# Where the tiles begin: one residue modulo 256 bytes for all of SBUF, another for the weights of the 256-column products

## The chip, the cores and the metric

The kernel runs on one core of a Trainium2 chip. The metric is device time in microseconds of one execution: before the change the median of three runs is 1165.34 us (1165.07 to 1167.91). One further execution was profiled; the rows shown below are from it.

## What is computed

A two-layer decoder trunk on 512 tokens of width 1024, in float32. Layer 0 mixes with a gated DeltaNet (six heads), layer 1 with a sliding-window attention (12 query heads, 2 key/value heads), both add an attention into 256 memory tokens, and both end in a feed-forward block of width 2816. The two feed-forward blocks hold most of the matrix work:

```python
def swiglu(h, w_gate_up, w_down):
    gu = h @ w_gate_up
    return (jax.nn.silu(gu[..., :D_FF]) * gu[..., D_FF:]) @ w_down

for layer in range(DEPTH):
    h = rms_norm(x, ln_mix[layer])
    ...
    x = x + jnp.concatenate([mix_out, mem_o], axis=-1) @ w_out[layer]
    x = x + swiglu(rms_norm(x, ln_ffn[layer]), w_gate_up[layer], w_down[layer])
    ...
return rms_norm(x, ln_final)
```

## The kernel before

Activations are kept transposed, features on the 128 partitions and the 512 tokens along the free dimension. Every float32 matrix product is made of three products of rounded operands: an operand is split into a high part (ScalarE, `copy` at L138) and the rest (VectorE, L151), and `mm3` adds high by high, high by low and low by high into one PSUM bank. In these products the weight part is the stationary operand (a 128 by 128 piece of a tile `whi` or `wlo`), and the activation part (`h`, `l`, `ac8h`, `T` and so on) streams through TensorE as the moving operand. Nearly all of TensorE's time is in two sizes of such products:

- **512 columns.** `project` (input projections, output projections, the first four gate tiles of a feed-forward block) and the down products of `ffn`, all into banks named `pj` (some `g` and `sc`). The weights come through `weight`, which takes a pair of tiles of 1024 columns from the pool `w`, three buffers each.
- **256 columns.** All other gate and up products of `ffn` go through `quarters`, which computes two column tiles of the weights by two halves of the tokens with seven products in place of eight. Each product is four `mm3`, twelve matmuls of 256 columns into a bank `g`. Its moving operands are halves of `h` or the sums of `token_sums` (tiles `T`). Its weights are split by `ring` into halves of the same `whi`/`wlo` tiles: a tile of 1024 columns holds two places of 512.

Two stretches of `quarters` lie in each feed-forward block, each followed by down products; at the end of layer 1 the last two down tiles are computed in token halves, so in 256 columns too.

**Where a tile lies.** Pools open on the left side of SBUF (`const`, `w`, `acta`, `actb`, `x`) grow upwards from the constants; pools opened on the right (`layer0`, `early`, `gdn`, `ffn0`, `swa`, `ffn1`) grow downwards from the top. A tile's length is rounded up to 32 bytes by the allocator, and nearly all large tiles are a multiple of 256 bytes long, so the few short ones decide the residue of all that follow. In the built program the tiles of `w`, `acta`, `actb` and `x` begin at 96 modulo 256, those on the right mostly at 224. A weight piece begins a multiple of 512 bytes into its tile, and a moving operand at its tile's beginning or 1024 bytes into it, so the residue of an operand is that of its tile:

| matmuls in high and low parts | moving operand | weights | count |
|---|---|---|---|
| 512 columns | 96 | 96 | 2112 |
| 512 columns (`ac8` to `ac11`, and the memory output of layer 0) | 224 | 96 | 324 |
| 256 columns (most of them on `T`) | 224 | 96 | 2028 |
| 256 columns (most of them on `h`) | 96 | 96 | 1488 |
| 256 columns (last down tile) | 96 | 224 | 144 |
| 256 columns (the rest) | 224 | 224 | 12 |

**The sum of squares.** For each RMS norm, `accumulate` squares a tile on ScalarE and adds it on VectorE to a running sum; each sum goes to the other of two buffers `sqa`. `rstd_from` sums it over the partitions with one matmul by ones.

**Smaller tiles.** `token_sums` keeps a column of negated gains (`minus`) and a half tile `fc`; `scores` and `weigh` keep `mx`, `den`, `nm`, `es`; `solve` keeps `Y32` and `Y64`, three buffers each. The order on each engine comes from the scheduler of the tile layer, which follows the program where nothing waits.

Of the kernel before, what the change touches and what calls it, by code (L numbers as in the profile page):

```python
# [18 lines left out]
P = 128  # L19
# [7 lines left out]
DFF = 2816  # L27
FT = DFF // P
EPS = 1e-6
NEG = -1e30  # L30
BASE = 32
NB = P // BASE
# [54 lines left out]
class Builder:  # L87
# [6 lines left out]
    def t(self, pool, shape, dtype=F32, tag=None, bufs=None, name=None):  # L94
        self.n += 1
        nm = f"{name or tag}_{self.n}"
        kw = {}
        if tag is not None:
            kw["tag"] = tag
        if bufs is not None:  # L100
            kw["bufs"] = bufs
        return pool.tile(shape, dtype, name=nm, **kw)

    @contextmanager
# [69 lines left out]
    def load(self, src, pool=None, bufs=2):  # L174
# [2 lines left out]
        self.nc.sync.dma_start(raw, src)  # L177
        return raw

    def weight(self, src, eng=None, raw=None, parts=1, pool=None, tags=("whi", "wlo"), bufs=3):  # L180

        raw = self.load(src) if raw is None else raw
        n = raw.shape[1]
        hi = self.t(pool or self.wpool, [P, D], F32R, tags[0], bufs)[:, :n]
        lo = self.t(pool or self.wpool, [P, D], F32R, tags[1], bufs)[:, :n]
        for i in range(parts):
            s = slice(i * n // parts, (i + 1) * n // parts)
            self.split(raw[:, s], hi[:, s], lo[:, s], eng or self.weng)
        return hi, lo
# [37 lines left out]
    def build(self):  # L227
        tc, nc, a = self.tc, self.nc, self.a
        with ExitStack() as st:
            opened = lambda name, **kw: tc.tile_pool(name=name, bufs=1, reuse_waits="tile", **kw)  # L230
            pool = lambda name, **kw: st.enter_context(opened(name, **kw))
            cp = pool("const")
            self.wpool, self.apool = pool("w"), pool("acta")
            self.dpool = pool("scratch", space=DRAM)
            self.load_constants(cp)
            self.weng = nc.vector
            with opened("layer0", side="right") as self.mpool:
                with self.banks(pj=3, g=2, sc=3):
                    with opened("early", side="right") as ep:
                        self.mem_and_norm(ep)  # L240
                        self.gates(ep)
                    with opened("gdn", side="right") as gp:
                        mix = self.gdn(gp)
                    self.bpool, xp = pool("actb"), pool("x")
                    self.x = [self.t(xp, [P, T], F32, f"x{k}") for k in range(KD)]
                    for k in range(KD):
                        nc.sync.dma_start(self.x[k], a["xT"][:, k, :])
                    self.rstd, self.cosT, self.sinT = (self.t(xp, [P, T], F32, n) for n in ("rstd", "cosT", "sinT"))
                    h = self.output(xp, 0, mix, self.bpool)
            with opened("ffn0", side="right") as fp, self.banks(pj=2, g=6):  # L250
                self.ffn(fp, xp, 0, h, self.apool, rope=True)
            with self.banks(pj=2, g=1, qk=1, pt=2, sc=1):
                with opened("swa", side="right") as sp:
                    mix = self.swa(sp)
                h = self.output(xp, 1, mix, self.apool)
            with opened("ffn1", side="right") as fp, self.banks(pj=2, g=6):
                self.ffn(fp, xp, 1, h, self.bpool)

    def load_constants(self, cp):
        nc, a = self.nc, self.a  # L260
        c = self.t(cp, [P, C_N], F32, "consts")
        g = self.t(cp, [P, G_N], F32, "gains")
        s = self.t(cp, [P, 24], F32, "small")
        nc.sync.dma_start(g, a["gains"])
        self.consts, self.gains, self.small = c, g, s
        self.ident = c[:, C_ID:C_ID + P]
        self.U = c[:, C_U:C_U + P]
        self.ones = c[:, C_ONE:C_ONE + P]
        self.caus = c[:, C_CAUS:C_CAUS + P]
        self.band = c[:, C_BAND:C_BAND + 2 * P]  # L270
        self.one = c[:, C_ONE:C_ONE + 1]
        v = self.t(cp, [P, 2], F32, "eps")
        nc.vector.memset(v[:, 0:1], EPS)
        nc.vector.memset(v[:, 1:2], EPS * EPS * P)
        self.eps, self.epsq = v[:, 0:1], v[:, 1:2]
# [376 lines left out]
    def solve(self, gp, heads, Ns, X64, Tts):  # L652

        nc = self.nc
        Xs = [X64[:, h * NC:(h + 1) * NC, :] for h in heads]
        part = lambda ps, a, w: ps[:, a * w * NC:(a + 1) * w * NC].rearrange("p (c m) -> p c m", c=NC)
        for B, starts in ((BASE, (0, 2 * BASE)), (2 * BASE, (0,))):
            pairs = [(slice(s, s + B), slice(s + B, s + 2 * B)) for s in starts]
            banks = [self.bank("sc") for _ in heads]
            ys = [self.t(gp, [P, NC, B], F32, f"Y{B}", 3) for _ in heads]  # L660
            for ps, N, X, y in zip(banks, Ns, Xs, ys):
                for a, b in pairs:
                    for c in range(NC):
                        self.mm(part(ps, 0, B)[b, c, :], N[a, c, b], X[a, c, 0:B])
                for a, b in pairs:
                    nc.vector.tensor_copy(y[b], part(ps, 0, B)[b])
            for ps, X, y, Tt in zip(banks, Xs, ys, Tts):
                for a, b in pairs:
                    for c in range(NC):
                        if B == BASE and a.start == 0:  # L670
                            self.mm(part(ps, 1, B)[b, c, :], Tt[b, c, b], y[b, c, :])
                        self.mm(part(ps, 2 if B == BASE else 1, B)[a, c, :], y[b, c, :], Tt[b, c, b])
                for a, b in pairs:
                    if B == BASE and a.start == 0:
                        self.ts(X[b, :, 0:B], part(ps, 1, B)[b], -1.0, ALU.mult)
                    self.ts(Tt[a, :, b], part(ps, 2 if B == BASE else 1, B)[a], -1.0, ALU.mult)
# [33 lines left out]
    def scores(self, pool, q, kk, win):  # L710
# [3 lines left out]
        half = [slice(0, 64), slice(64, P)]  # L714
        sm = [self.t(pool, [P, 2, 2, 2 * P], F32, "sm", 4 if own else 2) for _ in range(2)]
        sm = [t[:, n] for t in sm for n in range(2)]
        mx = self.t(pool, [P, 2 * NC], F32, "mx", 2)
        den = self.t(pool, [P, 2 * NC], F32, "den", 2)
        nm = self.t(pool, [P, 2 * NC], F32, "nm", 2)
        for n0 in range(0, NC, 2):  # L720
            if own:
                two = self.bank("qk", [P, 2, 2, 2 * P])
# [8 lines left out]
            for b in range(2):  # L731
# [14 lines left out]
        return sm, mx, den, nm  # L746

    def weigh(self, pool, scores, vv, m, out, sinks):

# [1 line left out]
        win = sinks is not None  # L751
        own = "pt" in self.pbufs
        half = [slice(0, 64), slice(64, P)]
        sm, mx, den, nm = scores
        if win:
            sk = sinks.unsqueeze(2).to_broadcast([P, 2, NC])
            v4 = lambda ap: ap.rearrange("p (b n) -> p b n", b=2)
            self.stt(v4(mx), v4(mx), 0.125, sk, ALU.mult, ALU.max)
            self.ts(nm, mx, -1.0, ALU.mult)
            es = self.t(pool, [P, 2 * NC], F32, "es", 2)  # L760
# [49 lines left out]
    def output(self, xp, layer, mix, hpool):  # L810
# [5 lines left out]
        for m in range(KD):  # L816
# [6 lines left out]
            self.acc = self.accumulate(xp, self.acc, self.x[m], m)  # L823
        return h

    def ffn(self, fp, xp, layer, h, apool, rope=False):
# [22 lines left out]
        def ring():  # L849

            if not places:
                for _ in range(3):
                    two = [self.t(self.wpool, [P, D], F32R, t, 3) for t in ("whi", "wlo")]
                    places.extend(tuple(x[:, i * T:(i + 1) * T] for x in two) for i in range(2))
            places.append(places.pop(0))
            return places[-1]

# [22 lines left out]
        for f0, half in ((0, 12), (12, 10)):  # L880
# [16 lines left out]
            for m in range(tail):  # L897
# [5 lines left out]
                        self.mm3(ps, w, k, acts[j + k], j + k == 0, j + k == half - 1)  # L903
                add(self.x[m], ps)
                if f0:
                    self.acc = self.accumulate(xp, self.acc, self.x[m], m)
                if rope and f0 == 0 and m == 0:
                    self.rope_tables(fp)
        if tail < KD:
# [9 lines left out]
            for t in parts:  # L919
                acc = self.acc[:, t]  # L920
                for m in range(tail, KD):
# [5 lines left out]
                    sq = self.t(fp, [P, T], F32, "fg", 4)[:, t]  # L927
                    self.square(sq, x)
                    if m < KD - 1:
                        nxt = self.t(xp, [P, T], F32, "sqa", 2)[:, t]  # L930
                        self.tt(nc.vector, nxt, acc, sq, ALU.add)
                        acc = nxt
                ends.append(self.final(fp, (acc, sq), t))
            for (ps, r), o, t in zip(ends, outs, parts):
                self.store(ps, r, o, t, tail)
# [1 line left out]
    def token_sums(self, fp, layer, j, h):  # L937
# [77 lines left out]
        self.mm(ps, self.ones, acc)  # L1015
        self.rsqrt(self.rstd[:, t], ps, D)

    def accumulate(self, pool, acc, x, m, out=None):

        n = x.shape[1]  # L1020
        sq = self.t(pool, [P, T], F32, "sq", 2)[:, :n]
        self.square(sq, x)
        if acc is None:
            return sq
        nxt = self.t(pool, [P, T], F32, "sqa", 2) if out is None else out
        self.tt(self.nc.vector, nxt, acc, sq, ALU.add)
        return nxt

    def rope_tables(self, pool):

# [192 lines left out]
```

## Time and profile before

| | us |
|---|---|
| median of the runs | 1165.34 |
| the profiled execution | 1165.44 |
| its span, first to last instruction | 1163.7 |
| TensorE (PE) busy | 1139.6 (98%) |
| weight loads (PEld) busy | 997.3 (86%) |
| VectorE (DVE) busy | 843.7 (73%) |
| ScalarE (ACT) busy | 635.8 (55%) |
| share of PE in the chain that ended last | 88% |

Matmuls are pipelined and their ends are modelled in the profile: a product of 256 columns is shown with a duration near 280 ns although the next one starts about 120 ns later. What a product costs is therefore read from how many of them follow each other in a piece of the chain, not from the mean duration of its group. The granted TensorE clock was 0.997 of full over the whole execution.

### The profile page before, as it was taken

Reading aid. Unit: us, or ns where it says so; the run is one execution under the profiler, and the core shown is the slowest. Engines: PE = TensorE matmul, PEld = TensorE weight load, DVE = VectorE, ACT = ScalarE, POOL = GpSimd, SP = SyncE. Lnnn points to the kernel's source line nnn. Section 1 sums busy time; section 2 is a strip of 40 time slices with the busy share of each in tenths; the row PEclk is TensorE's granted clock in tenths of the full one; section 3 lists DMA queues with packets and bytes.
Section 4 is the critical chain, followed back from the end, with each engine's and each line's share of the span. In section 5 each row is a group of like instructions: output and inputs, shape, how many; then the busy total and the mean of one; then the engine's idle time right before and its main releaser. Section 6 shows DMA issues by size and latency. Waiting matters only on the chain.

```text
span 1163.7 us, 19670 instructions
## 1 busy us (share of the span) xinstructions
PE 1139.6 (98%) x7476; PEld 997.3 (86%) x7476; DVE 843.7 (73%) x1587; ACT 635.8 (55%) x1273; POOL 85.9 (7%) x97
## 2 busy tenths in 40 slices
PE   7999999999999999999999999999999999999996
PEld 6888777877899998899998777678999988999986
DVE  5754877767789887378866767859799843898754
ACT  7569563366556652256654547675566522566533
POOL 0310000000101100011100000010011100111000
PEclk9999999999999999999999999999999999999998
DMA  8434352224657744567723421143477733577232
GB/s 307 135 101 115 113 127 92 74 90 163 170 142 187 183 127 124 148 148 179 182 70 102 136 73 38 55 107 124 106 187 185 186 108 103 141 182 187 70 93 94
DMA packets 73971, 152.83 MB, mean 131 GB/s; under 512 B 17756, under 2 KB 18420, under 8 KB 73876
## 3 DMA queue, kind: packets, MB, share of 16 engines
q1 hardware_dynamic: 62356, 130.59, 36.2%
q0 software_dynamic: 11520, 20.98, 11.7%
q8 instruction: 59, 0.97, 0.4%
q14 instruction: 36, 0.29, 0.1%
HBM read 144.58 MB, written 6.96 MB: 130 GB/s over the span
## 4 chain that ended last, share of the span: by engine, by line
PE 88%; DVE 7%; ACT 2%; DMA 1%; issue 1%; SPq 0%; DVEq 0%; ACTq 0%
PE pj L144 42%; PE g L144 39%; PE sc L144 5%; DVE wlo L151 2%; PE pt L148 1%; PE g L148 1%; ACT whi L138 1%; ACT sm L132 1%; DMA wraw<-in_wmk 1%; DVE sm L736 0%; DVE l L154 0%; DVE l L151 0%; PE qk L144 0%; DMA wraw<-in_win 0%; DVE q L151 0%
## 5 line engine op out<-in xcount | busy, mean ns | idle before, releaser
L138 ACT ACTIVATE whi<-wraw 128x512 fp32r<-128x512 f32 (+2 forms) x331 | 244.9, 746 | 272.5 <-PE pj L144 179.3
L151 DVE TENSOR_TENSOR wlo<-wraw,whi 128x512 fp32r<-128x512 f32 (+2 forms) x331 | 274.1, 837 | 108.3 <-ACT whi L138 102.4
L144 PE MATMUL pj<-h,whi 128*128 128x512 f32 (+1 forms) x676 | 266.1, 395 | 0.2
L144 PE MATMUL pj<-l,whi 128*128 128x512 f32 (+1 forms) x676 | 265.0, 392 | 0.3 <-DVE l L154 0.3
L144 PE MATMUL pj<-h,wlo 128*128 128x512 f32 (+1 forms) x676 | 265.0, 392 | 0.0
L144 PE MATMUL g<-T,whi 128*128 128x256 f32 x1280 | 232.1, 282 | 0.0
L144 PEld LDWEIGHTS g<-T,whi 128*128 128x128 f32 x1280 | 196.8, 189 | 1.5 <-DVE fu L154 1.5
L144 PE MATMUL g<-T,wlo 128*128 128x256 f32 x640 | 180.1, 281 | 0.0
L144 PEld LDWEIGHTS pj<-h,whi 128*128 128x128 f32 x676 | 127.0, 188 | 29.3 <-issue 3.1
L144 PEld LDWEIGHTS pj<-l,whi 128*128 128x128 f32 x676 | 127.0, 188 | 27.5 <-issue 2.0
L144 PEld LDWEIGHTS pj<-h,wlo 128*128 128x128 f32 x676 | 127.2, 188 | 26.6 <-issue 1.9
L144 PE MATMUL g<-h,wlo 128*128 128x256 f32 (+1 forms) x508 | 146.5, 288 | 0.0
L144 PE MATMUL g<-h,whi 128*128 128x256 f32 (+1 forms) x508 | 146.3, 288 | 0.0
L144 PE MATMUL g<-l,whi 128*128 128x256 f32 (+1 forms) x508 | 146.1, 288 | 0.0
L144 PEld LDWEIGHTS g<-T,wlo 128*128 128x128 f32 x640 | 120.4, 188 | 0.0
L144 PEld LDWEIGHTS g<-h,wlo 128*128 128x128 f32 x508 | 96.5, 190 | 1.2 <-issue 0.2
L144 PEld LDWEIGHTS g<-l,whi 128*128 128x128 f32 x508 | 96.5, 190 | 1.3
L144 PEld LDWEIGHTS g<-h,whi 128*128 128x128 f32 x508 | 96.5, 190 | 1.2
L972 POOL DMA_DIRECT2D ws<-in_wgu x40 | 35.6, 890 | 733.5 <-ACT sq L141 246.2
L138 ACT ACTIVATE whi<-ws 128x512 fp32r<-128x512 f32 x80 | 50.5, 631 | 52.6 <-PE g L144 43.2
L151 DVE TENSOR_TENSOR fu<-pj,rstd 128x512 f32<-128x512 f32 (+1 forms) x34 | 22.4, 659 | 55.8 <-PE pj L144 55.7
L151 DVE TENSOR_TENSOR wlo<-ws,whi 128x512 fp32r<-128x512 f32 x80 | 54.8, 685 | 7.3 <-ACT whi L138 7.2
(345 smaller groups left out, 1629.4 us busy)
## 6 DMA issues: line engine op xcount, KB each, us to landing
wraw<-in_wgu SPq DMA_DIRECT2D x48, 512.0 KB, 4.2
ws<-in_wgu SPq DMA_DIRECT2D x80, 256.0 KB, 3.6
ws<-in_wgu POOLq DMA_DIRECT2D x80, 256.0 KB, 4.8
wraw<-in_wdn SPq DMA_DIRECT2D x48, 384.0 KB, 3.2
wraw<-in_win SPq DMA_DIRECT2D x26, 512.0 KB, 3.7
wraw<-in_wgu SPq DMA_DIRECT2D x40, 256.0 KB, 4.3
wraw<-in_wout SPq DMA_DIRECT2D x16, 512.0 KB, 3.6
wraw<-in_wdn SPq DMA_DIRECT2D x16, 256.0 KB, 2.7
```

The costliest lines, as they stand in the source:

```text
L132: ins = self.nc.scalar.activation(out, in_, func, **kw).ins
L138: self.copied = self.nc.scalar.activation(out, in_, AF.Copy, **kw).ins
L144: return self.nc.tensor.matmul(out, lhsT, rhs, start=start, stop=stop, skip_group_check=more).ins
L148: return self.nc.tensor.transpose(out, in_, self.ident[:k, :k]).ins
L151: return eng.tensor_tensor(out=out, in0=a, in1=b, op=op).ins
L972: nc.gpsimd.dma_start(s1, a22, accum_op=ALU.add)
```

## The change

Six edits, all of them about where tiles lie or how many there are:

1. Every SBUF tile whose length is not a multiple of 64 bytes is made longer up to one (`t`), and a 32-byte tile is put at the outer end of the right side (`edge`). With the other edits all large tiles of both sides now begin at 192 modulo 256.
2. The weight tiles `whi`/`wlo` of the pool `w` are 64 columns (256 bytes) longer (`parts`, `SPARE`). `weight` still uses them from their beginning. `ring`, which serves the 256-column products, begins 16 columns (64 bytes, `SHIFT`) into them, at 0 modulo 256.
3. The running sum of squares is kept in one buffer `sqa` and added to in place; the first square is written straight into it.
4. `mx`, `den`, `nm` and `es` become rows of one tile `stats`.
5. `Y32` and `Y64` share three buffers `Y`; `fc` takes a buffer of the ring `fs`.
6. The two columns of negated gains move into the tile `eps` of the constants.

In the built program after, 3360 matmuls of 256 columns have their moving operand at 192 and their weights at 0 modulo 256; the other 312 of 256 columns (memory keys and values, and the halves at the end) and all 2436 of 512 columns have both at 192.

```diff
+LINE = 64
+SHIFT, SPARE = 16, 64
...
+        width = LINE // mybir.dt.size(dtype)
+        n = math.prod(shape[1:])
+        if pool.space not in (PSUM, DRAM) and n % width:
+            flat = pool.tile([shape[0], -(-n // width) * width], dtype, name=nm, **kw)[:, :n]
...
+    def parts(self):
+        return [self.t(self.wpool, [P, D + SPARE], F32R, t, 3) for t in ("whi", "wlo")]
+
     def weight(self, src, eng=None, raw=None, parts=1, pool=None, tags=("whi", "wlo"), bufs=3):
...
-        hi = self.t(pool or self.wpool, [P, D], F32R, tags[0], bufs)[:, :n]
-        lo = self.t(pool or self.wpool, [P, D], F32R, tags[1], bufs)[:, :n]
+        if pool is None:
+            hi, lo = (x[:, :n] for x in self.parts())
+        else:
+            hi, lo = (self.t(pool, [P, D], F32R, t, bufs)[:, :n] for t in tags)
...
+            pool("edge", side="right").tile([P, 8], F32, name="edge")
...
-        v = self.t(cp, [P, 2], F32, "eps")
+        v = self.t(cp, [P, 10], F32, "eps")
+        self.minuses = [v[:, 2 + 4 * i:6 + 4 * i] for i in range(2)]
...
-            ys = [self.t(gp, [P, NC, B], F32, f"Y{B}", 3) for _ in heads]
+            ys = [self.t(gp, [P, NC, 2 * BASE], F32, "Y", 3)[:, :, :B] for _ in heads]
...
-        mx = self.t(pool, [P, 2 * NC], F32, "mx", 2)
-        den = self.t(pool, [P, 2 * NC], F32, "den", 2)
-        nm = self.t(pool, [P, 2 * NC], F32, "nm", 2)
+        stats = self.t(pool, [P, 4, 2 * NC], F32, "stats", 2)
+        mx, den, nm, es = (stats[:, i, :] for i in range(4))
...
                 for _ in range(3):
-                    two = [self.t(self.wpool, [P, D], F32R, t, 3) for t in ("whi", "wlo")]
-                    places.extend(tuple(x[:, i * T:(i + 1) * T] for x in two) for i in range(2))
+                    two = self.parts()
+                    places.extend(tuple(x[:, SHIFT + i * T:SHIFT + (i + 1) * T] for x in two) for i in range(2))
...
-                        nxt = self.t(xp, [P, T], F32, "sqa", 2)[:, t]
-                        self.tt(nc.vector, nxt, acc, sq, ALU.add)
-                        acc = nxt
+                        self.tt(nc.vector, acc, acc, sq, ALU.add)
...
-            self.minus = self.t(fp, [P, 4], F32, "minus")
+            self.minus = self.minuses[layer]
...
-        c = self.t(fp, [P, q], F32, "fc")
+        c = self.t(fp, [P, q], F32, "fs", 3)
...
-    def accumulate(self, pool, acc, x, m, out=None):
-
-        n = x.shape[1]
-        sq = self.t(pool, [P, T], F32, "sq", 2)[:, :n]
-        self.square(sq, x)
-        if acc is None:
-            return sq
-        nxt = self.t(pool, [P, T], F32, "sqa", 2) if out is None else out
-        self.tt(self.nc.vector, nxt, acc, sq, ALU.add)
-        return nxt
+    def accumulate(self, pool, acc, x):
+
+        if acc is None:
+            acc = self.t(pool, [P, T], F32, "sqa", 1)
+            self.square(acc, x)
+            return acc
+        sq = self.t(pool, [P, T], F32, "sq", 2)
+        self.square(sq, x)
+        self.tt(self.nc.vector, acc, acc, sq, ALU.add)
+        return acc
```

TensorE's instructions stand in the same order before and after, and so do those of SyncE and GpSimd; on ScalarE a few rows change places at the start of the feed-forward blocks. VectorE's order changes at two kinds of places. The first is the start of the program, where `ml` is the low part of the memory tokens; before:

```order
1 L273 MEMSET eps_70 128x1
2 L274 MEMSET eps_70 128x1
3 L154 SCALAR_TENSOR_TENSOR ml_85<-mem_82,gains_67,mh_84 128x256 x2
4 L151 TENSOR_TENSOR wlo_137<-wraw_87,whi_136 128x512
5 L154 SCALAR_TENSOR_TENSOR ml_85<-mem_82,gains_67,mh_84 128x256 x2
```

and after:

```order
1 L290 MEMSET eps_70 128x1
2 L291 MEMSET eps_70 128x1
3 L168 TENSOR_SCALAR eps_70<-gains_67 128x4 x2
4 L164 SCALAR_TENSOR_TENSOR ml_89<-mem_86,gains_67,mh_88 128x256 x2
5 L161 TENSOR_TENSOR wlo_141<-wraw_91,whi_140 128x512
```

The two negations of gains have moved here from the beginning of the two feed-forward blocks. The second place is the token sums at the end of layer 0's output projection (`x` is the residual stream, `fu` the sums, `sqa` the running sum of squares); before:

```order
366 L151 TENSOR_TENSOR sqa_3036<-sqa_2996,sq_3034 128x512
367 L158 TENSOR_SCALAR minus_3125<-gains_67 128x4
368 L158 TENSOR_SCALAR fc_3127<-x_538_2741,gains_67 128x256
369 L154 SCALAR_TENSOR_TENSOR fu_3128<-x_538_2741,gains_67,fc_3127 128x256
370 L154 SCALAR_TENSOR_TENSOR fu_3129<-x_542_2745,gains_67,fc_3127 128x256
371 L154 SCALAR_TENSOR_TENSOR fu_3128<-x_542_2745,minus_3125,fu_3128 128x256
372 L158 TENSOR_SCALAR fc_3175<-x_539_2742,gains_67 128x256
```

and after:

```order
367 L161 TENSOR_TENSOR sqa_2796<-sqa_2796,sq_3029 128x512
368 L168 TENSOR_SCALAR fs_3119<-x_534_2741,gains_67 128x256
369 L168 TENSOR_SCALAR fs_3167<-x_535_2742,gains_67 128x256
370 L164 SCALAR_TENSOR_TENSOR fu_3120<-x_534_2741,gains_67,fs_3119 128x256
371 L164 SCALAR_TENSOR_TENSOR fu_3121<-x_538_2745,gains_67,fs_3119 128x256
372 L164 SCALAR_TENSOR_TENSOR fu_3120<-x_538_2745,eps_70,fu_3120 128x256
```

The half tile of the second sum (`fs_3167`) no longer waits for the first to be read, so it stands earlier; the add to `sqa` now reads and writes the same buffer.

More of the change, by code (lines that the diff above doesn't have):

```diff
@@ L101, in t @@
             kw["bufs"] = bufs
+        width = LINE // mybir.dt.size(dtype)
+        n = math.prod(shape[1:])
+        if pool.space not in (PSUM, DRAM) and n % width:
+            flat = pool.tile([shape[0], -(-n // width) * width], dtype, name=nm, **kw)[:, :n]
+            if len(shape) == 2:
+                return flat
+            names = "abcdef"[:len(shape) - 1]
+            return flat.rearrange(f"p ({' '.join(names)}) -> p {' '.join(names)}", **dict(zip(names, shape[1:])))
         return pool.tile(shape, dtype, name=nm, **kw)
@@ L745, in scores @@
                                 accum_out=den[:, i:i + 1])
-        return sm, mx, den, nm
+        return sm, mx, den, nm, es
     def weigh(self, pool, scores, vv, m, out, sinks):
@@ L753, in weigh @@
         half = [slice(0, 64), slice(64, P)]
-        sm, mx, den, nm = scores
+        sm, mx, den, nm, es = scores
         if win:
@@ L759, in weigh @@
             self.ts(nm, mx, -1.0, ALU.mult)
-            es = self.t(pool, [P, 2 * NC], F32, "es", 2)
             self.tt(nc.vector, v4(es), v4(nm), sk, ALU.add)
@@ L822, in output @@
             h.append(hl)
-            self.acc = self.accumulate(xp, self.acc, self.x[m], m)
+            self.acc = self.accumulate(xp, self.acc, self.x[m])
         return h
@@ L905, in ffn @@
                 if f0:
-                    self.acc = self.accumulate(xp, self.acc, self.x[m], m)
+                    self.acc = self.accumulate(xp, self.acc, self.x[m])
                 if rope and f0 == 0 and m == 0:
```

## The prediction

> **What bounds the kernel now.** I read the page first, for the engine that the end waits for.
>
> ```profile
> span 1163.7 us, 19670 instructions
> PE 1139.6 (98%) x7476; PEld 997.3 (86%) x7476; DVE 843.7 (73%) x1587; ACT 635.8 (55%) x1273; POOL 85.9 (7%) x97
> ...
> PE 88%; DVE 7%; ACT 2%; DMA 1%; issue 1%; SPq 0%; DVEq 0%; ACTq 0%
> ```
>
> TensorE is the bound, with 88% of the chain. The profiled execution took 1165.44 us, 0.10 above the median of the runs, so the sum below is made against 1165.4. Then I read the chain in order of time for its long pieces; the columns are start, length, and how many matmuls followed each other without a wait.
>
> ```profile
> 113.27 10.67 PE pj L144 x47
> ...
> 318.32 16.34 PE pj L144 x72
> 334.66 98.47 PE g L144 x828
> 435.91 64.86 PE pj L144 x283
> 500.76 98.45 PE g L144 x828
> ...
> 831.14 98.47 PE g L144 x828
> 932.38 64.84 PE pj L144 x283
> 997.22 98.46 PE g L144 x828
> ```
>
> Four pieces of 828 products of 256 columns hold 393.9 us, a third of the span, with no other engine in them: one product every 118.9 ns. The 512-column pieces give 226.9 ns (16.34 by 72) where both operands lie at 96 modulo 256, and 229.2 (64.86 by 283) in the down products, where a third of the moving operands lie at 224. So 256 further columns cost 226.9 - 118.9 = 108.0 ns: that is what streaming takes, and 10.9 ns per product, long or short, is something else. Anything that shortens it shortens the span directly, since these pieces wait for nothing.
>
> Third, whether a residue is seen in the spacing at all. The chain in four short windows: the first two within one down product of 36 matmuls, eight tiles at 96 and then `ac8` to `ac11` at 224, same weights tiles, same neighbours; the last two within `quarters`, a product on `h` (96) and then three on `T` (224).
>
> ```profile
> 470.29 2.72 PE pj L144 x12
> 473.23 2.79 PE pj L144 x12
> 340.86 1.32 PE g L144 x11
> 345.15 4.26 PE g L144 x36
> ```
>
> At 512 columns equal residues cost 226.7 ns and residues 128 apart 232.5, 5.8 more. At 256 columns it is the other way round: 120.0 ns at equal residues and 118.3 at 128 apart. So the 10.9 ns are, in part, the two reads of TensorE, moving operand and next weights, getting in each other's way in SBUF by address, and the offset that suits the long product does not suit the short one.
>
> [...]
>
> **The change part by part.** *Weights 64 bytes off, for 256 columns.* The products it reaches:
>
> ```profile
> L144 PE MATMUL g<-T,whi 128*128 128x256 f32 x1280 | 232.1, 282 | 0.0
> L144 PE MATMUL g<-T,wlo 128*128 128x256 f32 x640 | 180.1, 281 | 0.0
> L144 PE MATMUL g<-h,wlo 128*128 128x256 f32 x480 | 135.4, 282 | 0.0
> L144 PE MATMUL g<-h,whi 128*128 128x256 f32 x480 | 135.4, 282 | 0.0
> L144 PE MATMUL g<-l,whi 128*128 128x256 f32 x480 | 135.1, 281 | 0.0
> ```
>
> 1280 + 640 + 3 x 480 = 3360. No row shows an offset of 64. Bounds: below, the streaming alone, 108.0 ns; above, what the worse offset did to 512 columns, 5.8 ns more than now, 124.7. The nearest row is the one other offset that is shown at 256 columns, which lies 1.7 ns under the equal one, so the sign is a gain; for its size I take the middle between now and the streaming, 113.5 ns (an estimate). That is 5.4 ns by 3360 = 18.1 us. If the products stay where equal residues put them, 120.0, it is 3360 x 1.1 = 3.7 us lost.
>
> *One residue for the 512-column products.* The 324 products at 224 and 96 (`ac8` to `ac11`, and the memory output in layer 0) come to equal residues: 5.8 ns each, 1.9 us. This term is read off two rows of one stream and I keep it in every case but the one where residues do not matter.
>
> *All starts at multiples of 64 bytes.* Before, every moving operand of these products lies 32 bytes past such a multiple, so the trace can't show what an aligned one costs. Bounds: nothing, and the whole 10.9 ns of the 2112 others, 23.0 us. [...] I take nothing for it in the sum and make it a case of its own. [...]
>
> *Do the engines that feed these products keep up?* The windows of the four 256-column pieces (length, then busy time and count for PE, PEld, DVE, ACT, POOL) and two groups of VectorE within one of them:
>
> ```profile
> 334.66:433.13 98.47, 98.47 (x829) 98.47 (x829) 87.04 (x156) 61.33 (x118) 12.97 (x15) 1.00 0.67 167
> 500.76:599.21 98.45, 98.45 (x830) 98.45 (x829) 85.80 (x153) 61.94 (x118) 12.94 (x15) 1.00 0.65 155
> 831.14:929.61 98.47, 98.47 (x829) 98.47 (x829) 86.38 (x154) 61.33 (x118) 16.42 (x19) 1.00 0.75 181
> 997.22:1095.68 98.46, 98.46 (x830) 98.46 (x829) 85.82 (x153) 61.94 (x118) 12.97 (x15) 1.00 0.64 154
> ...
> L151 DVE TENSOR_TENSOR wlo<-wraw,whi 128x512 fp32r<-128x512 f32 x41 | 27.7, 690 | 4.8 <-ACT whi L138 3.5
> L151 DVE TENSOR_TENSOR wlo<-ws,whi 128x512 fp32r<-128x512 f32 x16 | 10.9, 684 | 1.2 <-ACT whi L138 1.2
> ```
>
> VectorE has 87.04 us of work in a piece; at 113.5 ns a piece takes 828 x 113.5 = 94.0 us, so VectorE would be 93% busy in place of 88%, still below. Its own time does not hang on residues: with both inputs at 96 (`wraw`, `whi`) the subtraction takes 690 ns, with one at 224 (`ws`) 684. The transfers' share goes from 0.75 at most to about 0.79.
>
> *The sum of squares in one buffer.* The add on VectorE is in order after the one before it in any case, and its other input is still one of two `sq`; the first square now writes `sqa` itself and must wait until the matmul by ones has read the last sum, which lies hundreds of microseconds back. The chain at the place where it is used is TensorE alone up to 318.32, where the next piece begins, so nothing of it was on the path. Cost nothing; if an add came late, VectorE's queue behind it holds the split of the next weights, and the loss would be one add of 0.69 us (the 128x512 row above), at each of five sums 3.5 us in all.
>
> *The smaller tiles.* Two negations go to the start of the program, ahead of the first low part:
>
> ```profile
> L158 DVE TENSOR_SCALAR minus<-gains x2: 158/174/189, 309.9 to 773.7; 128x4 f32<-128x4 f32 x2
> 6.96 0.69 DVE L151 TENSOR_TENSOR wlo<-wraw,whi 128x512 fp32r<-128x512 f32 x1
> ```
>
> They need the gains, which the rows behind them need too, and they take 0.35 us of a time when VectorE waits for the first loads (before 6.96 us it has only to wait). If that cover is gone they cost 0.35 us. `Y`, `fc` and `stats` add three waits of VectorE on its own earlier rows and none of TensorE on another engine; the three rows of `Y` (its copies) can start only when TensorE has done with the matmuls ahead, which also read the old contents. Cost nothing. No DMA is added, and the queues of SyncE and GpSimd keep their order.
>
> Sum: 18.1 + 1.9 = 20.0 us, 1165.4 - 20.0 = 1145.4 us.
>
> **The rivals.** *Aligned starts count too* (0.25). [...] With half of the 10.9 gone from 512 columns as well, 2112 x 5.4 = 11.4 and 324 x (5.8 + 5.4) = 3.6 us: 1165.4 - 18.1 - 11.4 - 3.6 = 1132 us. If all of it went, 3360 x 10.9 + 2112 x 10.9 + 324 x 16.7 = 65.0 us: 1100.
>
> *The reads do not collide* (0.08). The 512-column rows differ for another reason, say the pool `ac8` comes from; the time stays at 1165 us. [...]
>
> *The offset does nothing for 256 columns* (0.12). Their spacing would then be what loading 128 columns of weights per product allows: PEld is busy in all of the four pieces (98.47 of 98.47 us), in the 512-column piece not. Then only the 1.9 us of the 324 remain, or they are eaten by the 120.0 of equal residues: 1163.5 to 1167 us.
>
> *VectorE becomes the bound* (0.07). It decides from 87.04/828 = 105 ns per product if its work is perfectly spread; with its row waits of some 6 us per piece (4.8 and 1.2 in the rows above) from 112. Half of the gain comes back: 1155 us.
>
> *64 bytes is a worse offset* (0.13), the case on the other side. [...] It decides from 0.6 ns more per product than now (1.9 us by 3360). At 5.8 more: 1165.4 + 19.5 - 1.9 = 1183 us. For it: 512 columns show that an offset can hurt. Against: at 256 columns the only offset seen helps.
>
> **How the numbers follow.** The forecast has 0.35, with aligned starts 0.25, the rest as given. The range should leave out 2 in 10: at the top the worse offset (0.13) beyond 1168, at the bottom the part of the aligned case in which more than three quarters of it comes true, 1122 (0.07). 0.3%, about 3.5 us, is what a measurement of this kernel can tell from no change. Faster than 1161.8: 0.35 + 0.25 + 0.07 and a little of the cases about 1165, 0.70; within: 0.15; slower: 0.15, the worse offset and a little of the case with no effect.
>
> **What would show it.** Right: pieces of 828 matmuls in `g` of about 94 us, the piece of `ac8` to `ac11` at 2.72 us for 12, `pj` pieces still 226.9 ns per matmul, VectorE's groups unchanged at 684 to 690 ns. Wrong in the step on 64 bytes: `g` pieces of 98 us or more. Wrong on aligned starts: 72 matmuls of `pj` in clearly under 16.34 us. VectorE the bound: `g` pieces broken by waits on `wlo`.

## The result, and the profile after

The kernel after the change takes 1161.29 us (median of 6 runs, 1160.74 to 1162.59), the kernel before 1166.0 us in all runs of it up to then (6, 1165.07 to 1167.91). The ratio is 0.996, with a 95% interval of 0.9949 to 0.9971: faster by 0.4%, and clear of no change. The forecast had the sign right and the size wrong: 4.7 us in place of 20.0.

The profiled execution of after took 1162.59 us, its span is 1160.8 at a granted clock of 0.998. The page, first the busy times, then the shares of the chain:

```profile
span 1160.8 us, 19674 instructions
PE 1135.7 (98%) x7476; PEld 995.0 (86%) x7476; DVE 843.1 (73%) x1587; ACT 635.5 (55%) x1273; POOL 85.8 (7%) x97
...
PE 86%; DVE 8%; ACT 2%; DMA 2%; issue 1%; SPq 0%; DVEq 0%; ACTq 0%
```

The bound is the same, and TensorE's busy time is down by 3.9 us for the same 7476 matmuls. The long pieces of the chain of waits (start, length, matmuls without a wait between them; L154 is the line that was L144):

```profile
318.91 16.36 PE pj L154 x72
335.27 97.52 PE g L154 x828
435.53 64.17 PE pj L154 x283
499.70 97.52 PE g L154 x828
...
830.96 97.52 PE g L154 x828
931.25 64.17 PE pj L154 x283
995.42 97.52 PE g L154 x828
```

Each piece of 828 products of 256 columns is 0.93 to 0.95 us shorter: 117.8 ns a product for 118.9. Each down piece of 283 is 0.67 to 0.69 us shorter, 226.7 ns a product throughout for 229.2; the two other down pieces (206 and 244 products) lose 0.5 us together. That is 3.8 + 1.4 + 0.5 = 5.6 us. The 72 products at the top, which had equal residues before and have them still, take the same (16.36 for 16.34).

The span is down by 2.9 us only. Of the missing 2.7, 0.6 lie ahead of the first piece of 828, which begins at 335.27 in place of 334.66, and 2.1 between the first layer's last down piece and the third piece of 828. There the chain of after leaves TensorE:

```profile
778.54 7.96 DMA wraw<-in_wout
...
788.93 4.24 DMA wraw<-in_wout
```

Two loads of layer 1's output projection weights arrive late; before, the chain there is TensorE alone. The profiles of the experiments fall into two groups: from the end of the piece of 206 to the start of the next piece of 828 it is 182.2 to 182.3 us in the profiles of before and of experiments 2, 3, 7, 8 and 9, and 183.2 to 186.7 in those of after and of experiments 1, 4, 5, 6, 10 and 11. Kernels with hardly any difference in their code stand on both sides, so I count the wait to the execution, not to a term of the change; what decides it was not settled.

VectorE's rows did not change (684 ns in the piece of before, 685 here over the whole program):

```profile
L161 DVE TENSOR_TENSOR wlo<-ws,whi 128x512 fp32r<-128x512 f32 x80 | 54.8, 685 | 6.9 <-ACT whi L148 6.8
```

Two things in the traces do not fit the prediction's picture of a product of 108.0 ns and some further time that varies. The mean spacing is the same from one end of a piece of 828 products to the other (117.8 ns in each quarter of after's four), and where the stream starts again after a stall it can be shorter for a few products. The timeline just behind after's last piece of 828 (start, duration, matmul, count; durations overlap; the lines left out repeat those above them):

```profile
1094.34 0.39 PE L154 MATMUL g<-T,whi 128*128 128x256 f32 x2
1094.57 0.28 PE L154 MATMUL g<-T,wlo 128*128 128x256 f32 x1
...
1095.25 0.28 PE L154 MATMUL g<-T,wlo 128*128 128x256 f32 x1
1095.36 0.40 PE L154 MATMUL pj<-l,whi 128*128 128x512 f32 x1
```

Nine products start between 1094.34 and 1095.36, 113.3 ns apart on average, with the same kinds of operands, the same offset and the same granted clock (1.00 in the windows 1090 to 1094 and 1094.6 to 1096) as the 117.8 ahead of them. 120.0, the spacing at equal residues, is 6.7 more.

### The profile page after: what moved, and what is told of

Same layout as the page of the kernel before. It is cut to its first block, busy times and chain, and to the rows that moved or that the text cites. A ratio compares the mean times of both kernels' runs of the same rounds, so it can differ in the third digit from the quotient of the medians.

```text
span 1160.8 us, 19674 instructions
## 1 busy us (share of the span) xinstructions
PE 1135.7 (98%) x7476; PEld 995.0 (86%) x7476; DVE 843.1 (73%) x1587; ACT 635.5 (55%) x1273; POOL 85.8 (7%) x97
## 4 chain that ended last, share of the span: by engine, by line
PE 86%; DVE 8%; ACT 2%; DMA 2%; issue 1%; SPq 0%; DVEq 0%; ACTq 0%
PE pj L154 40%; PE g L154 38%; PE sc L154 6%; DVE wlo L161 2%; PE pt L158 1%; DMA wraw<-in_wout 1%; PE g L158 1%; ACT sm L142 1%; DVE l L164 1%; ACT whi L148 1%; DMA wraw<-in_wmk 1%; DVE btmp L161 1%; DVE big L161 0%; DVE sm L752 0%; PE qk L154 0%
## 5 line engine op out<-in xcount | busy, mean ns | idle before, releaser
L154 PE MATMUL pj<-h,whi 128*128 128x512 f32 (+1 forms) x676 | 266.4, 395 | 0.8 <-ACT h L148 0.5
L154 PE MATMUL pj<-l,whi 128*128 128x512 f32 (+1 forms) x676 | 265.2, 392 | 1.2 <-DVE l L164 1.2
L154 PE MATMUL pj<-h,wlo 128*128 128x512 f32 (+1 forms) x676 | 265.3, 393 | 0.0
L154 PE MATMUL g<-T,whi 128*128 128x256 f32 x1280 | 230.3, 282 | 0.0
L154 PEld LDWEIGHTS g<-T,whi 128*128 128x128 f32 x1280 | 197.6, 190 | 1.6 <-DVE fu L164 1.6
L154 PE MATMUL g<-T,wlo 128*128 128x256 f32 x640 | 180.1, 281 | 0.0
L154 PEld LDWEIGHTS pj<-h,whi 128*128 128x128 f32 x676 | 127.1, 188 | 29.7 <-issue 3.0
L154 PEld LDWEIGHTS pj<-l,whi 128*128 128x128 f32 x676 | 127.2, 188 | 28.4 <-DVE l L164 2.0
L154 PEld LDWEIGHTS pj<-h,wlo 128*128 128x128 f32 x676 | 127.3, 188 | 26.3 <-issue 1.9
L154 PE MATMUL g<-h,wlo 128*128 128x256 f32 (+1 forms) x508 | 146.2, 288 | 0.0
L154 PE MATMUL g<-l,whi 128*128 128x256 f32 (+1 forms) x508 | 146.1, 288 | 0.0
L154 PE MATMUL g<-h,whi 128*128 128x256 f32 (+1 forms) x508 | 146.0, 287 | 0.0
L154 PEld LDWEIGHTS g<-T,wlo 128*128 128x128 f32 x640 | 120.2, 188 | 0.0
L154 PEld LDWEIGHTS g<-l,whi 128*128 128x128 f32 x508 | 97.5, 192 | 1.2
L154 PEld LDWEIGHTS g<-h,whi 128*128 128x128 f32 x508 | 95.4, 188 | 1.2
L154 PEld LDWEIGHTS g<-h,wlo 128*128 128x128 f32 x508 | 95.4, 188 | 1.2 <-issue 0.2
```

The source lines that it names most:

```text
L154: return self.nc.tensor.matmul(out, lhsT, rhs, start=start, stop=stop, skip_group_check=more).ins
```

## The experiments

The theory after the result: **only the distance** between weights and moving operand modulo 256 bytes matters; a product of 256 columns takes 113.3 ns, or 6.67 more if its two reads collide, and the distance sets which share of the products collide. Its rivals: **aligned starts**, by which the gain comes in part from tiles that begin at multiples of 64 bytes; **the loads' own length**, by which 117.8 is what loading 128 columns of weights allows; and **the small edits** having brought or cost something themselves. The part about distance held: 117.8 and 226.7 ns with every start 32 bytes lower (experiment 4). The mean of a stream with one offset lies between the two times (115.6 to 120.0 ns), and single products do not keep to them (115 to 125 ns at 160 bytes); that reads collide was the author's picture, and no trace shows it.

### Offsets by stretch: experiments 1, 2, 5 and 9

A form of after in which each of the four stretches has an offset of its own, in floats, for its products of 256 columns (`QUARTERS`) and for its down products of 512 columns (`DOWN`). The form is the same in the four runs, the numbers differ.

```diff
+QUARTERS, DOWN = (0, 8, 24, 32), (8, 16, 32, 48)
...
-            hi, lo = (x[:, :n] for x in self.parts())
+            hi, lo = (x[:, shift:shift + n] for x in self.parts())
...
-                    places.extend(tuple(x[:, SHIFT + i * T:SHIFT + (i + 1) * T] for x in two) for i in range(2))
+                    places.extend(tuple(x[:, self.shift + i * T:self.shift + (i + 1) * T] for x in two) for i in range(2))
...
+            stretch = 2 * layer + (f0 > 0)
+            self.shift = QUARTERS[stretch]
```

**Experiment 1**, offsets 0, 32, 96 and 128 bytes; down products 32, 64, 128, 192.

> The kernel after, with the offset of the weights in the 256-column products set by stretch: 0, 32, 96 and 128 bytes in the four stretches of 828, and the weights of the four groups of down products (512 columns) at 32, 64, 128 and 192 bytes; nothing else is changed. Theory A, only the distance between weights and moving operand modulo 256 counts: the stretch at 0 takes 828 x 120.0 = 99.4 us, the one at 128 about 828 x 118.5 = 98.1 us as before the change, the down products at 128 go from 226.7 to 232.5 ns. Theory B, the absolute residues count as well: the stretch at 128 and the down products at 128 come out differently from before by more than 1 ns per product. Theory C, the spacing is set by what the other engines do to SBUF, not by TensorE's own two reads: all four stretches stay within 0.5 ns of 117.8 (97.5 us).

Measured 1169.14 us (one run). The long pieces of its chain:

```profile
334.92 99.35 PE g L155 x828
437.05 66.02 PE pj L155 x283
503.07 97.98 PE g L155 x828
...
835.15 97.16 PE g L155 x828
...
1000.87 98.26 PE g L155 x828
```

**Experiment 2**, offsets 160, 192, 224 and 16 bytes; down products 96, 160, 224, 16.

> As the sweep over low offsets, with 160, 192, 224 and 16 bytes in the four 256-column stretches, and the four groups of down products at 96, 160, 224 and 16 bytes. Theory A: the stretches differ from each other by more than 0.5 ns per product, and at least one offset lies under the 117.8 ns of 64 bytes, since one piece of twelve products after the change ran at 113; down products at 512 columns are worse than 226.7 at most offsets. Theory C: all within 0.5 ns of 117.8, and all down products at 226.7.

Measured 1168.22 us (one run):

```profile
335.17 99.35 PE g L155 x828
...
503.59 97.53 PE g L155 x828
...
834.06 96.60 PE g L155 x828
...
999.49 97.98 PE g L155 x828
1100.08 49.16 PE pj L155 x244
```

**Experiment 5**, offsets 208, 240, 216 and 232 bytes; down products 240, 208, 248, 8.

> As the first two sweeps, with 208, 240, 216 and 232 bytes in the four 256-column stretches (around 224, the best so far with 116.7 ns), and the four groups of down products at 240, 208, 248 and 8 bytes (around the equal residue, the best so far). If the spacing is a smooth function of the distance, 216 and 232 lie within 0.5 ns of 116.7. If it is the share of products that meet one collision (means between 113.3, which one piece of twelve products held, and the 120.0 of the settled equal residue), it moves by more than that with 8 bytes, and some offset may reach 113.3, a stretch of 93.8 us. Down products: above 226.7 at every offset but 0 if collisions count, 226.7 near 0 if it is smooth.

Measured 1165.67 us (one run):

```profile
334.89 96.60 PE g L155 x828
434.29 64.15 PE pj L155 x283
498.43 94.34 PE g L155 x805
...
829.74 99.34 PE g L155 x828
```

**Experiment 9**, offsets 8, 4, 248 and 200 bytes; down products 236, 244, 4, 200.

> As the other sweeps, with 8, 4, 248 and 200 bytes in the four 256-column stretches, and the four groups of down products at 236, 244, 4 and 200 bytes. Theory of whole collisions (each product takes 113.3 ns, or 6.7 more when its reads collide once; the offset sets only what share collides): every stretch's mean lies from 113.3 to 120.0 (93.8 to 99.4 us), and the down products near 226.7 or 233.3 ns or a mix, none under 220. A smooth dependence on the distance: 4 and 8 bytes within 0.5 ns of the 120.0 of no offset.

Measured 1163.28 us (one run):

```profile
334.64 95.69 PE g L155 x828
433.12 65.56 PE pj L155 x283
498.68 97.98 PE g L155 x828
```

Length by count gives, for 256 columns, the mean spacing at each offset. What it lies above 113.33 ns is then put as a part of one step of 6.67 ns:

| offset, bytes | mean ns per product | part of the step above 113.33 |
|---|---|---|
| 0, 160, 216 | 120.0 | 1 |
| 128 | 118.7 | 4/5 |
| 4, 16, 32 | 118.3 | 3/4 |
| 64, 192, 200, 232 | 117.8 | 2/3 |
| 248 | 117.6 | |
| 96, 240 | 117.2 to 117.3 | 3/5 |
| 208, 224 | 116.7 | 1/2 |
| 8 | 115.6 | 1/3 |

All but one are simple fractions, which a smooth dependence on the distance would not give: 208 and 224 bytes give 116.7, 216 between them 120.0, and 4 and 8 bytes 118.3 and 115.6. The fractions belong to the mean of a repeating group of products, though, and not to a share of products that lose the whole step. At 160 bytes (experiment 2) the part is 1, so every product should take 120.0; the timeline there:

```profile
400.16 0.29 PE L155 MATMUL g<-h,whi 128*128 128x256 f32 x1
400.29 0.28 PE L155 MATMUL g<-l,whi 128*128 128x256 f32 x1
400.40 0.28 PE L155 MATMUL g<-h,wlo 128*128 128x256 f32 x1
400.53 0.28 PE L155 MATMUL g<-h,whi 128*128 128x256 f32 x1
400.64 0.28 PE L155 MATMUL g<-l,whi 128*128 128x256 f32 x1
```

The starts lie 0.13 and 0.11 us apart in turn. Taken to the nanosecond in the trace, the gaps run 121, 117, 125, 115, 124, 118 in the middle of the stretch and begin again. In experiment 3 (0 bytes, the same mean) 826 of the 827 gaps of a piece are 120, and in after, at 64 bytes, all lie from 116 to 120 and none at 113.3. How the delay is dealt out within a group stays open.

The first sweep's other readings: the stretches differ by up to 2.7 ns, where its theory C allowed 0.5 from 117.8, and 128 bytes gives 118.7 ns, and 232.4 in the down products, as before the change within 1 ns and at other addresses (its theory A). The 512-column products are the other way about: 226.7 ns at 0 and at 240, 229 to 234 at the other offsets. So 0, the best distance for the long product, is the worst for the short one, as the prediction had read (240 is the one tried that is fair for both, which the expectation of experiment 5 had not foreseen), and the sizes between two measured offsets can't be interpolated.

### Experiment 3: the offset taken away

All six edits, but the products of 256 columns at equal residues too.

```diff
-SHIFT, SPARE = 16, 64
+SHIFT, SPARE = 0, 64
```

> The kernel after with the 64-byte offset taken out, everything at 192 modulo 256. Theory A: the four stretches run at 120.0 ns per product as the settled equal-residue products did before, 3360 x 2.2 = 7.4 us more than after, about 1168.7 us, so slower than before the change by some 2.5 us. Theory C: as after, 1161.3 us.

Measured 1168.07 us (median of 10 runs, 1166.98 to 1170.02) beside 1166.08 before (13 runs), ratio 1.0018 (1.0008 to 1.0027). Its four pieces of 828 are alike, here the first, and the down piece is that of after:

```profile
334.80 99.35 PE g L154 x828
436.94 64.17 PE pj L154 x283
```

Without the offset, one residue for all makes the kernel slower than before, since the kernel before had the offset of 128 in most products on `T`, by accident. The offset of 64 is worth 6.8 us against this kernel (3360 x (120.0 - 117.8) = 7.4 by the pieces), and only 3.8 by the pieces against before.

### Experiment 4: the same distances, 32 bytes lower

Every large tile begins at 160 in place of 192, the shifted weights at 224: 32 bytes past a multiple of 64.

```diff
-            pool("edge", side="right").tile([P, 8], F32, name="edge")
+            pool("edge", side="right").tile([P, 16], F32, name="edge")
...
-        g = self.t(cp, [P, G_N], F32, "gains")
+        g = cp.tile([P, G_N], F32, name="gains")
```

> The kernel after with every large tile moved down by 32 bytes: moving operands at 160 modulo 256, weights of the 256-column products at 224, so all starts 32 bytes past a multiple of 64 while the distances are kept. Theory A: no change, 117.8 and 226.7 ns per product, 1161.3 us within 1.5 us. Theory B (starts at multiples of 64 bytes save a line): 1 ns or more per product worse, 1165 us or more.

Measured 1161.14 us (4 runs, 1160.04 to 1161.88), ratio 0.9961 (0.9946 to 0.9976), as after:

```profile
334.85 97.52 PE g L154 x828
435.11 64.17 PE pj L154 x283
```

To the hundredth of a microsecond the pieces of after. Moving every start by 32 bytes at the same distances changes nothing (1161.14 us beside 1161.29): the rival of aligned starts falls. The line in its theory was the author's guess; no run shows one.

### Experiment 6: high and low parts at offsets of their own

Offsets in bytes of the high and the low part, by stretch: (224, 64), (224, 192), (64, 224), (96, 224).

```diff
+QUARTERS, DOWN = ((56, 16), (56, 48), (16, 56), (24, 56)), (0, 0, 0, 0)
...
-                    places.extend(tuple(x[:, SHIFT + i * T:SHIFT + (i + 1) * T] for x in two) for i in range(2))
+                    places.extend(tuple(x[:, s + i * T:s + (i + 1) * T] for x, s in zip(two, self.shift)) for i in range(2))
```

> The kernel after with different offsets for the high and the low weight tiles of the 256-column products: 224 and 64, 224 and 192, 64 and 224, 96 and 224 bytes in the four stretches. If each product's time hangs on its own weights' distance alone, the means are those of the single offsets weighted two to one (224: 116.7, 64 and 192: 117.8, 96: 117.4): 117.0, 117.1, 117.4, 117.1 ns. If it hangs on where the product before left the two reads, the means differ from these by more than 0.3 ns.

Measured 1161.24 us (one run):

```profile
334.35 98.73 PE g L155 x828
...
500.02 97.52 PE g L155 x828
...
830.11 96.92 PE g L155 x828
```

119.2, 117.8, 117.1 and (fourth piece, 97.52) 117.8 ns. Two thirds of the products use the high part; if each took what its own offset takes alone, all four would lie between 117.0 and 117.4. The first lies 2.2 above that. So what a product takes does not hang on its own weights' offset alone, and the table above holds for a stream with one offset, not for a product by itself.

### Experiment 7: narrower weight loads

Half of the products of 256 columns load 128, 96, 64 or 32 columns of weights, by stretch. It leaves out the contributions to the other output rows in those products.

```diff
+COLS = 128, 96, 64, 32
...
-                self.mm3(ps, w, j, sums[j][b], first and j == 0, j == 3, not first)
+                self.mm3(ps, w, j, sums[j][b], first and j == 0, j == 3, not first, self.cols if j in (1, 2) else P)
```

> The kernel after with fewer weight columns in six of the twelve matmuls of each 256-column product (the second and third 128 rows): 128, 96, 64 and 32 columns in the four stretches; the other output rows get no contribution from them. If the 10.9 ns beyond streaming come from the reads of the weights colliding with the moving operand's, or from the weight load itself being as long as the product, the narrowed matmuls go from 117.8 towards 108 to 111 ns, and a stretch of 828 from 97.5 to 93 or 94 us at 32 columns. If they are a fixed cost of changing weights, all four stretches stay at 97.5 us.

Measured 1153.55 us (one run). The four pieces:

```profile
334.58 97.52 PE g L155 x828
...
499.02 88.47 PE g L155 x780
...
824.77 97.98 PE g L155 x828
...
989.71 91.25 PE g L155 x805
```

117.8, 113.4, 118.3 and 113.4 ns. With 64 columns it is worse than with 128, so the length of the load does not set the spacing; but with 96 and with 32 the whole piece, the products with full loads in it too, settles at 113.4, and nowhere lower. That is the floor of the short window in after, and no run shows the 108.0 of the prediction for 256 columns. What makes up the floor was not found. Two figures bear on it and point different ways: 512 columns take just twice as long at their best (226.7 ns), as if the columns that stream set it; but early in after sixteen products of only 128 columns, each with a load of 128 columns, take 1.78 us, 111 ns each, so with a full load a product that is half as long is hardly shorter.

### Experiment 8: the small edits alone

Edits 3 to 6 on the kernel before; the tile at the outer end of the right side is sized so that the distances of before stay.

```diff
+            pool("edge", side="right").tile([P, 56], F32, name="edge")
```

> The kernel before with the other four edits alone (one buffer for the sum of squares, stats in one tile, Y and fc in shared buffers, negated gains in the constants), with padding that keeps every distance between weights and moving operand as it was (0 and 128). If these edits cost nothing: as before, 1166.0 us within 1.5. If they lose what the rows of the changed kernel do not account for: 1 to 2 us slower than before.

Measured 1167.03 us (10 runs, 1165.33 to 1169.55) beside 1165.76 (13 runs), ratio 1.001 (1.0001 to 1.002). Its pieces of 828 are those of before, 98.45 to 98.47 us. The loss of 1.2 us is barely clear of nothing, its profiled span (1164.0) is 0.3 above that of before, and no row shows a place for it.

### Experiments 10 and 11: better offsets

After, with 224 and with 8 bytes in place of 64.

```diff
-SHIFT, SPARE = 16, 64
+SHIFT, SPARE = 56, 64
```

> The kernel after with 224 bytes in place of 64 as the offset of the weights in the 256-column products, the best of the first two sweeps: 116.7 for 117.8 ns, 3360 x 1.1 = 3.7 us less than after, 1157.6 us. If the spacing hung on the stretch in which an offset was tried and not on the offset, the four stretches differ and the time stays at 1161.

Measured 1158.35 us (5 runs, 1157.5 to 1160.84), ratio 0.9931 (0.9917 to 0.9944). Its pieces run at 116.6 to 116.7 ns, as in the sweep; two of them end 48 and 23 products early. The first two:

```profile
334.59 96.60 PE g L154 x828
...
498.15 91.02 PE g L154 x780
```

```diff
-SHIFT, SPARE = 16, 64
+SHIFT, SPARE = 2, 64
```

> The changed kernel with an offset of 8 bytes in the place of 64, all else as it is. Theory of whole collisions (a product takes 113.3 ns or 6.67 ns more, and the offset sets the share that collide, one in three at 8 bytes by the fourth sweep, two in three at 64): the four pieces of 828 products take 95.7 us each in the place of 97.52, 115.6 ns for 117.8, so 3360 products by 2.2 ns, 7.4 us, are gone against the changed kernel's 1161.3: 1153.9 us, up to 3 us more where waits on VectorE's splits, which show in the run with 224 bytes, end pieces early. Theory that the share at an offset hangs on the stretch it was seen in and not on the offset alone: only the piece in the first layer's front half takes 95.7 us, the others 96.6 to 98, and the time is 1157 to 1161 us.

Measured 1154.91 us (5 runs, 1153.23 to 1156.52) beside 1165.14 (8 runs), ratio 0.9905 (0.9891 to 0.9919). The four pieces, and the end of the second one:

```profile
336.27 95.69 PE g L154 x828
...
498.94 93.71 PE g L154 x811
...
828.39 95.69 PE g L154 x828
...
991.05 92.96 PE g L154 x805
```

```profile
584.92 7.73 PE g L154 x67
592.65 0.02 issue
592.67 0.96 DVE wlo L161
593.63 0.34 DVE fu L161
```

All four stretches take 115.5 to 115.6 ns, so what an offset does is the same in every stretch. It is the fastest version tried, 6.4 us under after and 10 under before. The theory's sum was 7.4 under after; from the start of each piece to the down products behind it 7.0 are gone (98.48 for 100.26 in the first stretch, 98.41 for 100.11 in the second, and likewise in layer 1), the other 0.4 stay in stalls: the second and fourth pieces now end 17 and 23 products early, in a wait on VectorE's splits. The median shows 6.4 of the 7.0; the rest lies outside these stretches and was not followed.

## Why the prediction was wrong

**The bound and the sign** were right: the pieces wait for nothing, and most of what the products lost in them is gone from the time. Of the 5.6 us taken off TensorE's pieces the median shows 4.7. The sign was in part luck: it was read off one other offset, 128, and with 0, 160 or 216 bytes the 256-column products would have become slower than before.

**The term of 64 bytes** is the step that failed: "for its size I take the middle between now and the streaming, 113.5 ns". It was 117.8, so 1.1 ns by 3360, 3.8 us, in place of 5.4 ns and 18.1 us. The signs set beforehand left this case out: pieces of about 94 us for right, 98 or more for wrong, and they came at 97.52. Three things were wrong with that middle.

- Its lower end. 108.0, the difference between a long and a short product, was read as streaming, and the 10.9 ns above it as open to address. A product of 512 columns takes 226.7 at its best, which is two floors of 113.3: 108.0 came from subtracting a short stream that pays most of the step (118.9) from a long one near its least (226.9), and no run shows it. By the lowest steady spacing of any run at most 118.9 - 113.3 = 5.6 ns were to be had, so the middle alone would have been 2.8.
- The middle as a guess between two ends. The means jump from one offset to the next, on simple fractions of 6.67 ns above 113.3: 64 bytes leaves two thirds of the step, where the mix before had 5/6 (5.56 of 6.67), and only the runs could tell.
- The mix before. The windows of 11 and 36 products gave 120.0 and 118.3, and I took 118.9 as a thing to improve on. 128, which most products on `T` had, is one of the poorer offsets, but better than none: the kernel before was already 0.9 us a piece better than equal residues (experiment 3).

**The 324 products** behaved as read: 226.7 ns in the whole down piece. The pieces of 283, 206 and 244 lost 1.9 us together, about the 1.9 forecast.

**The reads do not collide** had 0.08, with the time at 1165 us; it came to 1161.29. With nothing but the distance changed, the same 828 products take 99.35, 97.52 or 95.69 us (experiments 3 and 11 beside after), and at one distance narrower loads change the spacing too (113.4 ns with 96 columns for 117.8 with 128, experiment 7). That it is the two reads that meet in SBUF is argued from this; no trace shows a read.

**Aligned starts** had 0.25, and fell in experiment 4 (97.52 us a piece with starts at multiples of 64 bytes and 32 bytes past them). It was the largest chance that I gave without a row behind it, and it alone pulled the range down to 1122. **VectorE as the bound** did not appear at 97.52 us a piece; waits on the splits begin to end the second and fourth pieces early at 117.3 ns a product (experiment 5, 805 of 828), and do so at 116.7 and 115.6 (experiments 10 and 11), so somewhat above the 112 that I had worked out for it. **No effect** and **a worse offset** were both possible in kind: 160 and 216 bytes would have cost 3360 x 1.1 = 3.7 us against before, not 19.5: no offset tried gave more than 120.0.

**The small edits** were costed at nothing; alone they measured 1.2 us slower, at the edge of what can be told, and within the bounds that I had given (3.5 and 0.35 us). With 5.6 us gained in the pieces they may be what the median lacks, but no row shows it. The edit of the running sum was not tried by itself.

## What to carry to other kernels

Where the spacing of products hangs on where their operands lie, find the lowest steady spacing in the long pieces of the chain (length by count) before interpolating: it says what is left to gain. A mean that is a simple fraction of a step does not show that single products take the whole step or none of it; that is read from their starts, one by one. An effect of addresses that jumps from one offset to the next (116.7, 120.0 and 116.7 ns at 208, 216 and 224 bytes) is measured and not reasoned out; a form of the kernel with another offset in each stretch gives four points for one run, and four such runs found the offset with which the kernel is 10 us faster than before, where with the argued one it is 4.7. Before an offset is priced, find out what the kernel has by accident.

## What the runs showed of the hardware

The spacing of float32 products in rounded parts, each with a load of 128 columns of weights, hangs on the distance of the two operands' addresses modulo 256 bytes, down to steps of 4 bytes (4, 8 and 16 bytes: 118.3, 115.6, 118.3 ns); 256 bytes more make no difference (the weight tiles of after begin 17 x 256 = 4352 bytes apart, and all gaps in its four pieces lie from 116 to 120 ns). It does not hang on the addresses themselves, as far as a shift of everything by 32 bytes tells (1161.14 us with it, 1161.29 without). At a granted clock of 0.996 to 0.998 the mean of a stream of 256-column products lies between 115.6 and 120.0 ns, for all distances tried but one (248 bytes) a simple fraction of 6.67 ns above the 113.3 that the stream holds with loads of 96 or 32 columns in half of the products. Single products spread around the mean in a repeating pattern (115 to 125 ns at 160 bytes, where the mean is 120.0). A stream keeps its mean over hundreds of products (117.8 ns in each quarter of a piece of 828 in after), and a few products after a stall may run faster (nine at 113.3 beside 117.8). Narrower weights change the mean in no order: 117.8 ns with 128 columns, 113.4 with 96, 118.3 with 64, 113.4 with 32.
